# Stick-breaking attention of a hybrid decoder layer: weights as beta times a scanned product of (1 - beta), in place of sums of logarithms on TensorE

## The chip, the cores and the metric

One core of one Trainium2 chip runs the whole layer. The metric is the device time of one execution in microseconds (us). PE is TensorE, DVE is VectorE, ACT is ScalarE, POOL is GpSimd, SP is SyncE, which issues most loads.

## The reference, cut to what matters

The layer has three token mixers in parallel (sliding-window attention with 8 heads, stick-breaking attention with 8 heads, attention to a memory of 256 tokens), each with a sigmoid gate and a projection, then an output projection and a SwiGLU feed-forward. There are 512 tokens, width 1024, heads of 64. The change is in the second mixer (nb = 4 blocks of 128 queries):

```python
def stick_breaking_attention(q, k, v):
    """A[t,s] = beta_ts * prod_{s<j<t}(1-beta_tj), s<t."""
    ...
        z = jnp.einsum('bqhd,bkhd->bhqk', q[:, i * BLOCK:L], k[:, :L]).astype(jnp.float32) * (d ** -0.5)
        t = i * BLOCK + jnp.arange(BLOCK)[:, None]
        causal = jnp.arange(L)[None, :] < t
        log_1m = jnp.where(causal, jax.nn.log_sigmoid(-z), 0.0)
        between = lax.cumsum(log_1m, axis=3, reverse=True) - log_1m
        a = jnp.where(causal, jnp.exp(jax.nn.log_sigmoid(z) + between), 0.0)
        outs.append(jnp.einsum('bhqk,bkhd->bqhd', a.astype(v.dtype), v[:, :L]))
```

beta is the sigmoid of the score z. A query at t gives the key at s the weight beta(t,s) times the product of 1 - beta over all keys between s and t.

## The kernel before

Nearly all products are made in float32r, with each operand split into a high and a low part (`split`: ACT casts `raw` to `hi`, DVE subtracts to get `lo`); `mm3` issues hi x hi, hi x lo and lo x hi. `mm` issues a single product.

Two things are interleaved in the middle part of the program. One is the stream `dn`: a list of weight units (projections `ka`, `qa`, gates `g1`, queries `qm`, memory keys `pmk`, memory values `pmv`, branch projections `br`), each loaded 4 units ahead by SP, split 3 units ahead, and multiplied on PE by a generator that yields an estimated time after each `mm3`. The other is the attention heads, generators too, that yield how many us of the stream are to stand at this place: `for us in sb_head(h): dn.run(us)`. A scheduler then sets each engine's order; `tc.high_priority()` and `after` (an order between two instructions without a wait) steer it. `dn.until(flag)` runs the stream up to a mark. ACT's functions come in table sets; `table(name)` loads one, ordered behind all earlier `fn` calls, and later ones stand behind it.

A stick-breaking head before the change has keys on the partitions and queries along the free axis. There are 10 blocks of 128x128 under the causal mask, in three PSUM banks `z` (SEG and W give place and width). PE makes the scores and adds a mask of -1e30 (`negm`). ACT makes |z|, then exp, then ln(1 + ...), DVE adds max(z, 0): this is the softplus, the negative logarithm of 1 - beta. DVE splits it into `sh` and `sl`. After 7.0 us of stream, PE adds the sums over later keys into `z`: with a triangle of -1 (`ntri`) inside a block and with a square of -1 (`none`) for whole blocks. ACT takes exp, which gives the weights with the keys on partitions, as the product with the values needs them. After 3.0 us of stream, and for odd heads only, PE multiplies the weights of the head pair with the values into `ysb`, and `pair_out` splits the result.

All eight heads run with ACT's set of logarithm and exponential. Behind them the stream runs to the end of the branch's gates, `sigmoids(SB)` loads the sigmoid set, takes the sigmoid of the gates and the first set comes back for the sliding-window softmax.

Of the kernel before, what the change touches and what calls it, by code (L numbers as in the profile page):

```python
# [17 lines left out]
P = 128  # L18
# [85 lines left out]
def tile_kernel(ctx, tc, a):  # L104
# [62 lines left out]
    def mm3(out, l, r, start, stop, right_last=False):  # L167
        (lh, ll), (rh, rl) = l, r
        one = nc.tensor.matmul(out, lh, rh, start=start, stop=False, skip_group_check=True)  # L169
        two, three = ((ll, rh), (lh, rl)) if right_last else ((lh, rl), (ll, rh))  # L170
        nc.tensor.matmul(out, *two, start=False, stop=False, skip_group_check=True)  # L171
        return one, nc.tensor.matmul(out, *three, start=False, stop=stop, skip_group_check=True)  # L172
# [373 lines left out]
    def mem_keys(i):  # L546
        def gen(hi, lo):
            if i % 2 == 0:
                st[("mk", i // 2)] = ck(f"mk{i}")
            t = st[("mk", i // 2)][:, (i % 2) * M : (i % 2 + 1) * M]  # L550
            ps = dps(f"pmk{i}")
            for k in range(KC):
                mm3(ps[:, :M], cols((hi, lo), k * P, P), mu[k], k == 0, k == KC - 1)
                yield 0.325
            nc.vector.tensor_tensor(t, ps[:, :M], st["mrb"][:, :], op=ALU.mult)
            if i % 2 == 1:
                st[("mks", i // 2)] = parts(f"mks{i // 2}", st[("mk", i // 2)])

        return gen

    def mem_vals(q):
        def gen(hi, lo):
            if q == 0:
                st["mrs"] = per_token("m", st["mrb"], M, dps)
                st["pmv"] = [dps(f"pmv{t}") for t in range(2)]
            for i in range(2):
                k = 2 * q + i
                for t in range(2):
                    x = (mu[k][0][:, t * P : (t + 1) * P], mu[k][1][:, t * P : (t + 1) * P])
                    mm3(st["pmv"][t][:, :], x, cols((hi, lo), i * 512, 512), k == 0, k == KC - 1)  # L570
                    yield 0.65
                    if k == KC - 1:
                        vt = ck(f"mv{t}")
                        nc.vector.tensor_scalar(
                            vt[:, :], st["pmv"][t][:, :], st["mrs"][:, t : t + 1], None, op0=ALU.mult
                        )
                        st[("mvs", t)] = parts(f"mvs{t}", vt)

        return gen
# [153 lines left out]
    ntri = const("ntri", [P, P])  # L733
# [7 lines left out]
    ntri_r = cst.tile([P, P], F32R, name="ntri_r")  # L741
    nc.gpsimd.tensor_copy(ntri_r[:, :], ntri[:, :])
    none = cst.tile([P, P], F32, name="none")
    nc.gpsimd.memset(none[:, :], -1.0)
    none_r = cst.tile([P, P], F32R, name="none_r")
    nc.gpsimd.tensor_copy(none_r[:, :], none[:, :])
# [19 lines left out]
    def band_bias():  # L766
# [10 lines left out]
        )  # L777
        ps = aps("pbias")
# [15 lines left out]
        return out  # L794


    SEG = [(0, 0, 512), (1, 0, 384), (2, 0, 256), (2, 256, 128)]
    W = [512, 384, 384]
# [5 lines left out]
    def sb_head(h):  # L804
        c = h // 2
        ks, qs, ql = (st[(x, c, h % 2)] for x in ("kbs", "qbs", "qbl"))
        z = [aps(f"z{h}{i}") for i in range(3)]

        def seg(ts, j):
            i, o, n = SEG[j]  # L810
            return ts[i][:, o : o + n]

        for j in range(4):
            i, o, n = SEG[j]
            kj = slice(j * P, (j + 1) * P)
            if j < 3:
                out, qh, qlo = z[i][:, o : o + n], qs[:, j * P :], ql[:, j * P :]
            else:

                out = z[i][:, o : o + 2 * n]  # L820
                qh = qs[:, j * P :].unsqueeze(1).to_broadcast([P, 2, P])
                qlo = ql[:, j * P :].unsqueeze(1).to_broadcast([P, 2, P])
            mm(out, ks[:, kj], qh, j < 3, False)
            mm(out, ks[:, kj], qlo, False, False)
        for i, o, n in SEG:
            mm(z[i][:, o : o + P], identb[:, :], negm[:, :], False, False)
        e = [ck(f"e{h}{i}") for i in range(3)]
        sh = [ck(f"sh{h}{i}", F32R) for i in range(3)]
        sl = [ck(f"sl{h}{i}", F32R) for i in range(3)]
        for i in range(3):  # L830
            x, n = e[i][:, : W[i]], W[i]
            nc.scalar.activation(x, z[i][:, :n], AF.Abs)
# [3 lines left out]
            if i == 2:  # L836

                nc.vector.tensor_tensor(e[i][:, 384:], e[i][:, 128:256], e[i][:, 256:384], op=ALU.add)
                x, n = e[i][:, :], 512
            nc.vector.tensor_copy(sh[i][:, :n], x)  # L840
            nc.vector.tensor_tensor(sl[i][:, :n], x, sh[i][:, :n].bitcast(F32), op=ALU.subtract)
        yield 7.0

        def both(t):

            return t[2][:, :].rearrange("p (b n) -> p b n", b=4)[:, 0:4:3, :]
# [12 lines left out]
        for i in range(3):  # L859
            last = fn(e[i][:, : W[i]], z[i][:, : W[i]], AF.Exp)  # L860
        yield 3.0
        if h % 2 == 0:
            st["even"] = e
            return

        ys = aps(f"ysb{c}")
        for j in range(4):
            for i, x in enumerate((st["even"], e)):
                ins = mm(ys[64 * i : 64 * i + 64, j * P :], vcols(j, 128 + (2 * c + i) * 64), seg(x, j), j == 0, j == 3)
                after(ins, last)  # L870
                last = ins
        pair_out(SB, c, ys)

# [4 lines left out]
    def swa_pair(c, bias):  # L878
        hs = (c, c + 4)
        s, w, pt, pts = {}, {}, {}, {}  # L880
        for i, h in enumerate(hs):
            qs, ks, kl = st[("qas", c, i)], st[("kas", 0, i)], st[("kal", 0, i)]
            s[h] = [aps(f"s{h}{i}") for i in range(2)]
            for n in (1, 0, 2, 3):
                q = slice(n * P, (n + 1) * P)
                if n == 0:
                    kh = ks[:, :P].unsqueeze(1).to_broadcast([P, 2, P])
                    klo = kl[:, :P].unsqueeze(1).to_broadcast([P, 2, P])
                else:
                    keys = slice((n - 1) * P, (n + 1) * P)  # L890
                    kh, klo = ks[:, keys], kl[:, keys]
                mm(blocks(s[h], n), qs[:, q], kh, n in (1, 2), False)
                mm(blocks(s[h], n), qs[:, q], klo, False, True)
        for h in hs:
            b = bias[h // 2][:, (h % 2) * 256 : (h % 2) * 256 + 256]
            w[h] = [ck(f"w{h}{i}") for i in range(2)]
            nc.gpsimd.memset(w[h][0][:, :P], NEG)
            nc.vector.tensor_tensor(w[h][0][:, P:256], s[h][0][:, P:256], b[:, P:256], op=ALU.add)
            nc.vector.tensor_tensor(w[h][0][:, 256:], s[h][0][:, 256:], b, op=ALU.add)
            nc.vector.tensor_tensor(  # L900
                w[h][1][:, :].rearrange("p (n k) -> p n k", n=2),
                s[h][1][:, :].rearrange("p (n k) -> p n k", n=2),
# [19 lines left out]
        for h in hs:  # L922

            pt[h] = [aps(f"pt{h}{i}") for i in range(2)]
            for n in range(NT):
                for e in range(2):
                    j = n - 1 + e
                    if j < 0:
                        continue
# [3 lines left out]
            nc.scalar.copy(pts[h][0][:, :], pt[h][0][:, :])  # L933
            nc.vector.tensor_copy(pts[h][1][:, :384], pt[h][1][:, :384])
        yield 2.0
        ys = aps(f"ysw{c}")
        for j in range(NT):
            n = 256 if j < 3 else P
            for i, h in enumerate(hs):
                mm(ys[64 * i : 64 * i + 64, j * P : j * P + n], vcols(j, i * 64), blocks(pts[h], j)[:, :n], j == 0, j == 3)  # L940
# [50 lines left out]
    table("sigmoid_and_others")  # L991
    sigmoids(SB)
# [534 lines left out]
def _constants():  # L1527
# [16 lines left out]
def _layout(i):  # L1544
# [5 lines left out]
    x, mem = i["x"][0], i["mem"][0]  # L1550
# [57 lines left out]
```

## Time and profile before

| what | value |
|---|---|
| median of 3 runs | 806.78 us (806.52 to 806.88) |
| the profiled execution | 806.6 us |
| its span on the core | 804.8 us |
| granted TensorE clock | 0.998 |
| PE, DVE, ACT, POOL busy | 99%, 77%, 59%, 10% of the span |
| eight stick-breaking heads with the stream between | from about 79 to 208 us |

The profile page gives busy times, the chain of work that ended last and the costliest groups; answers of the trace give single instructions in order of time (start, duration), waits, and busy times by stretch. PE's instructions overlap: the time that one costs is read from its start to the start of the next.

### The profile page before, as it was taken

What the parts mean: (1) busy time and instruction counts of PE and PEld (TensorE: products, weight loads), DVE (VectorE), ACT (ScalarE), POOL (GpSimd) and SP (SyncE); (2) the same over time, 40 slices, a digit from 0 to 9 for tenths busy, and PEclk for the clock granted to TensorE, in tenths of its full rate; (3) what the DMA queues carried; (4) which work ended last, traced back from release to release, by engine and by line L of the source; (5) the groups of instructions that cost most, each with busy time, mean ns of one, the idle gap of its engine ahead of it and who ended that gap; (6) DMA issues with size and microseconds to landing.
All of it is one profiled execution on the core that took longest, in us unless ns stands there. A gap on an engine that the chain in (4) does not pass through costs nothing.

```text
span 804.8 us, 12915 instructions
## 1 busy us (share of the span) xinstructions
PE 795.6 (99%) x4939; PEld 708.2 (88%) x4939; DVE 616.2 (77%) x983; ACT 477.0 (59%) x861; POOL 78.9 (10%) x101
## 2 busy tenths in 40 slices
PE   9999999999999999999999999999999999999996
PEld 6899788878788889889988899999999999988885
DVE  6898678646377888796694779967676767898787
ACT  7466677666756555754662566554444444666673
POOL 1002210000000000100004200100000000205200
PEclk9999999999999999999999999999999999999999
DMA  9343355211241404704669927987777662859802
GB/s 320 118 148 105 125 176 149 87 53 53 80 105 53 106 26 133 182 27 132 187 234 305 224 45 172 257 222 205 190 176 191 174 167 69 190 129 225 204 2 104
DMA packets 41726, 117.68 MB, mean 146 GB/s; under 512 B 4768, under 2 KB 6320, under 8 KB 41664
## 3 DMA queue, kind: packets, MB, share of 16 engines
q1 hardware_dynamic: 31584, 87.77, 33.9%
q0 software_dynamic: 9648, 28.82, 19.2%
q8 instruction: 38, 0.62, 0.3%
q10 hardware_dynamic: 432, 0.27, 0.1%
q14 instruction: 24, 0.20, 0.1%
HBM read 113.18 MB, written 3.67 MB: 145 GB/s over the span
## 4 chain that ended last, share of the span: by engine, by line
PE 95%; DVE 2%; ACT 1%; issue 1%; DMA 1%; DVEq 0%; ACTq 0%
PE gx L172 5%; PE gx L169 5%; PE gx L171 5%; PE z L175 4%; PE g L169 3%; PE br L169 3%; PE br L171 3%; PE g L171 3%; PE g L172 3%; PE br L172 3%; PE x L172 2%; PE x L171 2%; PE x L169 2%; PE gy L171 2%; PE gy L169 2%; PE gy L172 2%
## 5 line engine op out<-in xcount | busy, mean ns | idle before, releaser
L135 ACT CAST hi<-gw 128x1024 fp32r<-128x1024 f32 x77 | 79.9, 1048 | 81.4 <-DVE gw L1193 39.8
L136 DVE TENSOR_TENSOR lo<-gw,hi 128x1024 fp32r<-128x1024 f32 x77 | 93.5, 1223 | 34.1 <-ACT hi L135 34.0
L135 ACT CAST hi<-raw 128x1024 fp32r<-128x1024 f32 (+2 forms) x52 | 53.0, 1031 | 50.8 <-PE qb L171 11.3
L136 DVE TENSOR_TENSOR lo<-raw,hi 128x1024 fp32r<-128x1024 f32 (+2 forms) x52 | 63.0, 1217 | 20.1 <-ACT hi L135 19.9
L1175 POOL DMA_DIRECT2D gw<-in_w_gu x27 | 23.3, 895 | 190.4 <-DMA gw<-in_w_gu 81.4
L135 ACT CAST hi<-r 128x1024 fp32r<-128x1024 f32 (+1 forms) x24 | 23.5, 981 | 19.9 <-PE y L172 5.3
L171 PE MATMUL x<-lo,lh 128*128 128x512 f32 x88 | 34.3, 389 | 0.0
L169 PE MATMUL x<-hi,lh 128*128 128x512 f32 x88 | 34.2, 389 | 0.0
L172 PE MATMUL x<-hi,ll 128*128 128x512 f32 x88 | 34.1, 389 | 0.0
L136 DVE TENSOR_TENSOR lo<-r,hi 128x1024 fp32r<-128x1024 f32 (+1 forms) x24 | 27.1, 1130 | 4.0 <-ACT hi L135 3.9
L135 ACT CAST hi<-qw 128x1024 fp32r<-128x1024 f32 x18 | 18.9, 1051 | 16.0 <-PE g L171 3.9
L136 DVE TENSOR_TENSOR lo<-qw,hi 128x1024 fp32r<-128x1024 f32 x18 | 21.9, 1219 | 8.4 <-ACT hi L135 8.4
L835 DVE SCALAR_TENSOR_TENSOR e<-z,e 128x384 f32<-128x384 f32 (+1 forms) x24 | 14.3, 598 | 17.7 <-ACT e L188 17.7
L188 ACT ACTIVATE e<-e 128x384 f32<-128x384 f32 (+1 forms) x48 | 26.9, 561 | 1.6
L135 ACT CAST hi<-bp 128x512 fp32r<-128x512 f32 x33 | 19.3, 620 | 13.6 <-PE y L172 4.8
L136 DVE TENSOR_TENSOR lo<-bp,hi 128x512 fp32r<-128x512 f32 x33 | 22.1, 702 | 5.7 <-ACT hi L135 5.6
L172 PE MATMUL gx<-N2h,lo 128*128 128x256 f32 x88 | 25.0, 284 | 0.3 <-DVE lo L136 0.3
L169 PE MATMUL gx<-B11h,hi 128*128 128x256 f32 x88 | 25.1, 285 | 0.2 <-ACT B11h L1104 0.2
L169 PE MATMUL mx<-woh,mgh 128*128 128x512 f32 x64 | 25.0, 391 | 0.0
L172 PE MATMUL gw<-B21h,lo 128*128 128x256 f32 x88 | 25.0, 284 | 0.0
L171 PE MATMUL gx<-B11l,hi 128*128 128x256 f32 x88 | 25.0, 284 | 0.0
L172 PE MATMUL mx<-woh,mgl 128*128 128x512 f32 x64 | 24.9, 390 | 0.0
(920 smaller groups left out, 2967.5 us busy)
## 6 DMA issues: line engine op xcount, KB each, us to landing
gw<-in_w_gu SPq DMA_DIRECT2D x57, 512.0 KB, 5.1
gw<-in_w_gu POOLq DMA_DIRECT2D x27, 512.0 KB, 7.4
raw<-in_w_p SPq DMA_DIRECT2D x26, 512.0 KB, 4.3
qw<-in_w_p SPq DMA_DIRECT2D x15, 512.0 KB, 4.1
raw<-in_w_br SPq DMA_DIRECT2D x12, 512.0 KB, 3.8
bp<-in_w_dn SPq DMA_DIRECT2D x22, 256.0 KB, 8.7
r<-in_w_dn POOLq DMA_DIRECT2D x10, 512.0 KB, 8.1
raw<-in_w_out SPq DMA_DIRECT2D x8, 512.0 KB, 4.4
```

The lines of the kernel that those rows point to most:

```text
L135: ins = nc.scalar.copy(hi, raw)
L136: lows = nc.vector.tensor_tensor(lo, raw, hi.bitcast(F32), op=ALU.subtract)
L169: one = nc.tensor.matmul(out, lh, rh, start=start, stop=False, skip_group_check=True)
L171: nc.tensor.matmul(out, *two, start=False, stop=False, skip_group_check=True)
L172: return one, nc.tensor.matmul(out, *three, start=False, stop=stop, skip_group_check=True)
L175: return nc.tensor.matmul(out, l, r, start=start, stop=stop, skip_group_check=True)
L188: ins = nc.scalar.activation(*args, **kw)
L835: nc.vector.scalar_tensor_tensor(x, z[i][:, :n], 0.0, x, op0=ALU.max, op1=ALU.add)
L1175: nc.gpsimd.dma_start(gw[(n, key)][:, :], g_src(n, i, j), accum_op=ALU.add)
```

## The change

Queries go on the partitions and keys along the free axis, and all tokens are stored last first (the input's rows are reversed on the host and the output's back). The keys before a query then stand to its right, nearest first, and the product over the keys between is a running product along the free axis.

- Scores: the same products with the sides swapped. The narrowest block, once made 256 wide by repeating its 128 columns, is now 128 wide. The mask stays.
- ACT makes r = sigmoid(-z) and b = sigmoid(z), straight from PSUM. DVE scans r into a running product `p` (`tensor_tensor_scan`: state times r, then the maximum with `anew`, which is 0 but for a 1 where the second block of a bank begins anew), and multiplies b by the product one column before.
- The weights now have queries on the partitions. PE transposes the ten blocks (`at`), ordered behind the last `mm3` of the stream piece ahead of them, and ACT and DVE copy them to SBUF with priority. The product with the values follows as before, last key block first.
- The triangle and the minus ones, `sh` and `sl`, and their products go.
- The sigmoid set is loaded ahead of head 0, once the stream has made the memory norm, whose logarithm and exponential need the other set. The gates of this branch are then evacuated from PSUM through the sigmoid at once.
- The relative bias of the sliding window is loaded at head 0 and spread out at head 2 instead of all at head 1; the window blocks are mirrored. Memory keys and values are evacuated with priority, and the stream's price for a product of the keys is 0.37 instead of 0.325.

```diff
-    SEG = [(0, 0, 512), (1, 0, 384), (2, 0, 256), (2, 256, 128)]
-    W = [512, 384, 384]
+    SEG = [(0, 0, 512), (1, 0, 384), (2, 0, 256), (1, 384, 128)]
+    W = [512, 512, 256]
+    KEYS = [(1, 384, 128), (2, 0, 256), (1, 0, 384), (0, 0, 512)]
...
-            mm(out, ks[:, kj], qh, j < 3, False)
-            mm(out, ks[:, kj], qlo, False, False)
...
-        for i in range(3):
-            x, n = e[i][:, : W[i]], W[i]
-            nc.scalar.activation(x, z[i][:, :n], AF.Abs)
-            fn(x, x, AF.Exp, scale=-1.0)
-            st["chain"] = fn(x, x, AF.Ln, bias=1.0)
-            nc.vector.scalar_tensor_tensor(x, z[i][:, :n], 0.0, x, op0=ALU.max, op1=ALU.add)
...
-            nc.vector.tensor_copy(sh[i][:, :n], x)
-            nc.vector.tensor_tensor(sl[i][:, :n], x, sh[i][:, :n].bitcast(F32), op=ALU.subtract)
+        for n in range(NT):
+            i, o, w = SEG[n]
+            for x, first in ((qs, n < 3), (ql, False)):
+                mm(z[i][:, o : o + w], x[:, n * P : (n + 1) * P], ks[:, n * P :], first, False)
+        for n in (0, 1, 3, 2):
+            i, o, w = SEG[n]
+            mm(z[i][:, o : o + P], identb[:, :], negm[:, :], False, n > 1 or n == 0)
+        for i, w in enumerate(W):
+            fn(r[i][:, :w], z[i][:, :w], AF.Sigmoid, scale=-1.0)
+        for i, w in enumerate(W):
+            st["chain"] = fn(b[i][:, :w], z[i][:, :w], AF.Sigmoid)
+        for i, w in enumerate(W):
+            o = P if i == 1 else 0
+            p = ck(f"p{h}{i}")
+            nc.vector.tensor_tensor_scan(p[:, :w], r[i][:, :w], anew[:, o : o + w], 1.0, op0=ALU.mult, op1=ALU.max)
+            nc.vector.tensor_tensor(b[i][:, 1:w], b[i][:, 1:w], p[:, : w - 1], op=ALU.mult)
         yield 7.0
...
-        for j in range(2):
-            for t in (sh, sl):
-                mm(seg(z, j), ntri_r[:, :], seg(t, j), False, False)
-        for t in (sh, sl):
-            mm(z[2][:, :384], ntri_r[:, :], t[2][:, :384], False, t is sl)
-        for t in (sh, sl):
-            mm(z[0][:, 128:], none_r[:, :], seg(t, 1), False, False)
-        for t in (sh, sl):
-            mm(z[0][:, 256:], none_r[:, :], both(t), False, t is sl)
-            mm(z[1][:, 128:384], none_r[:, :], both(t), False, t is sl)
-        mm(z[2][:, 128:256], none[:, :], seg(e, 3), False, True)
-        for i in range(3):
-            last = fn(e[i][:, : W[i]], z[i][:, : W[i]], AF.Exp)
+        for n in (0, 1, 3, 2):
+            i, o, _ = SEG[n]
+            for j in range(n, NT):
+                t, c, _ = KEYS[j]
+                last = nc.tensor.transpose(
+                    pt[t][:, c + n * P : c + (n + 1) * P], b[i][:, o + (j - n) * P : o + (j - n + 1) * P], ident[:, :]
+                )
+                after(last, st["product"])
+        with tc.high_priority():
+            nc.scalar.copy(at[0][:, :], pt[0][:, :])
+            nc.vector.tensor_copy(at[1][:, :], pt[1][:, :])
+            nc.scalar.copy(at[2][:, :256], pt[2][:, :256])
         yield 3.0
...
+    while "mrb" not in st:
+        dn.piece()
+    table("sigmoid_and_others")
+    sigmoids(SB)
     for h in range(8):
-        if h == 1:
-            bias = band_bias()
+        if h == 0:
+            biases = band_bias()
+        if h in (0, 2):
+            bias = next(biases)
         for us in sb_head(h):
             dn.run(us)
     st.pop("chain")
     dn.until(f"gates{SB}")
-    table("sigmoid_and_others")
-    sigmoids(SB)
     table("natural_log_exp_and_others")
```

The order on three engines shows it. First PE in the second half of head 3, after the 7.0 us of stream. Before (`z_1427` to `z_1429` are the three score banks; moving operand first, then the stationary one):

```order
L175 MATMUL z_1427<-sh_1445,ntri_r 128x512
L175 MATMUL z_1427<-sl_1448,ntri_r 128x512
L175 MATMUL z_1428<-sh_1446,ntri_r 128x384
L175 MATMUL z_1428<-sl_1449,ntri_r 128x384
L175 MATMUL z_1429<-sh_1447,ntri_r 128x384
L175 MATMUL z_1429<-sl_1450,ntri_r 128x384
L175 MATMUL z_1427<-sh_1446,none_r 128x384
L175 MATMUL z_1427<-sl_1449,none_r 128x384
L175 MATMUL z_1427<-sh_1447,none_r 128x256
L175 MATMUL z_1428<-sh_1447,none_r 128x256
...
L175 MATMUL z_1429<-e_1444,none 128x128
L169 MATMUL qa_1527<-n0h,hi_1414 128x512
```

With the change (`at` are the turned weights in PSUM, `b` the weights):

```order
L172 MATMUL qa_1504<-n2h,lo_1399 128x512
L835 MATMUL at_1515<-c_ident,b_1429 128x128
L835 MATMUL at_1516<-c_ident,b_1429 128x128
L835 MATMUL at_1515<-c_ident,b_1429 128x128
L835 MATMUL at_1514<-c_ident,b_1429 128x128
L835 MATMUL at_1516<-c_ident,b_1430 128x128
L835 MATMUL at_1515<-c_ident,b_1430 128x128
L835 MATMUL at_1514<-c_ident,b_1430 128x128 x2
L835 MATMUL at_1515<-c_ident,b_1431 128x128
L835 MATMUL at_1514<-c_ident,b_1431 128x128
L169 MATMUL qa_1504<-n3h,hi_1398 128x512
```

Ten transposes stand where thirteen products stood (two of these, with `sl`, are left out above). Those that read the third weight tile come last.

Second, DVE in head 1. Before (`lo` is a weight's low part; `e` the softplus):

```order
L835 SCALAR_TENSOR_TENSOR e_1086<-z_1071,e_1086 128x512
L840 CAST sh_1089<-e_1086 128x512
L841 TENSOR_TENSOR sl_1092<-e_1086,sh_1089 128x512
L835 SCALAR_TENSOR_TENSOR e_1087<-z_1072,e_1087 128x384
L840 CAST sh_1090<-e_1087 128x384
L841 TENSOR_TENSOR sl_1093<-e_1087,sh_1090 128x384
L835 SCALAR_TENSOR_TENSOR e_1088<-z_1073,e_1088 128x384
L838 TENSOR_TENSOR e_1088<-e_1088 128x128
L840 CAST sh_1091<-e_1088 128x512
L136 TENSOR_TENSOR lo_1125<-raw_1002,hi_1124 128x1024
L841 TENSOR_TENSOR sl_1094<-e_1088,sh_1091 128x512
```

With the change (the scans are the rows that write `p`; `mk` are the memory keys):

```order
L826 SCALAR_TENSOR_TENSOR p_1103<-r_1094,anew 128x512
L826 SCALAR_TENSOR_TENSOR p_1106<-r_1095,anew 128x512
L827 TENSOR_TENSOR b_1091<-b_1091,p_1103 128x511
L827 TENSOR_TENSOR b_1092<-b_1092,p_1106 128x511
L826 SCALAR_TENSOR_TENSOR p_1109<-r_1096,anew 128x256
L136 TENSOR_TENSOR lo_1135<-raw_1057,hi_1134 128x1024
L557 TENSOR_TENSOR mk_1138<-pmk_1139,rb_m 128x256
L827 TENSOR_TENSOR b_1093<-b_1093,p_1109 128x255
```

Three scans and three products take the place of ten passes; a weight's low part and the memory keys stand ahead of the third product.

Third, ACT ahead of head 0. Before (`v_all` are the values, `t_m` and `rb_m` the memory norm):

```order
L508 COPY v_all<-pv_727 128x320
L832 ACTIVATE e_917<-z_902 128x512
L188 ACTIVATE e_917<-e_917 128x512 x2
L832 ACTIVATE e_918<-z_903 128x384
L188 ACTIVATE e_918<-e_918 128x384 x2
L832 ACTIVATE e_919<-z_904 128x384
L188 ACTIVATE e_919<-e_919 128x384 x2
L135 CAST hi_947<-raw_837 128x1024
L135 CAST hi_1004<-raw_945 128x1024
L188 ACTIVATE t_m<-ss_m,eps_t 128x256
L188 ACTIVATE rb_m<-t_m 128x256
```

With the change:

```order
L509 COPY v_all<-pv_722 128x320
L135 CAST hi_899<-raw_832 128x1024
L189 ACTIVATE t_m<-ss_m,eps_t 128x256
L189 ACTIVATE rb_m<-t_m 128x256
L197 ACT_TABLE_LOAD
L189 ACTIVATE r_955<-z_937 128x512
L189 ACTIVATE r_956<-z_938 128x512
L189 ACTIVATE r_957<-z_939 128x256
L189 ACTIVATE b_952<-z_937 128x512
L189 ACTIVATE b_953<-z_938 128x512
L189 ACTIVATE b_954<-z_939 128x256
```

The memory norm and a table load moved ahead of head 0's functions.

More of the change, by code (lines that the diff above doesn't have):

```diff
@@ L171, in mm3 @@
         nc.tensor.matmul(out, *two, start=False, stop=False, skip_group_check=True)
-        return one, nc.tensor.matmul(out, *three, start=False, stop=stop, skip_group_check=True)
+        st["product"] = nc.tensor.matmul(out, *three, start=False, stop=stop, skip_group_check=True)
+        return one, st["product"]
     def mm(out, l, r, start, stop):
@@ L740, in tile_kernel @@
     nc.gpsimd.tensor_copy(negm[:, :], nmf[:, :])
[L741 to L746, printed above, removed]
+    anew = cst.tile([P, 640], F32, name="anew")
+    nc.gpsimd.memset(anew[:, :], 0.0)
+    nc.gpsimd.memset(anew[:, 512:513], 1.0)
     def normed(k):
@@ L793, in band_bias @@
             out.append(b)
[L794 to L798 removed]
+        yield out
+    SEG = [(0, 0, 512), (1, 0, 384), (2, 0, 256), (1, 384, 128)]
+    W = [512, 512, 256]
+    KEYS = [(1, 384, 128), (2, 0, 256), (1, 0, 384), (0, 0, 512)]
     def pair_out(b, c, ps):
@@ L804, in sb_head @@
     def sb_head(h):
-        c = h // 2
-        ks, qs, ql = (st[(x, c, h % 2)] for x in ("kbs", "qbs", "qbl"))
+        c0 = h // 2
+        ks, qs, ql = (st[(x, c0, h % 2)] for x in ("kbs", "qbs", "qbl"))
         z = [aps(f"z{h}{i}") for i in range(3)]
[L809 to L822, printed above, removed]
-            mm(out, ks[:, kj], qh, j < 3, False)
-            mm(out, ks[:, kj], qlo, False, False)
@@ new lines, in sb_head @@
+        b = [ck(f"b{h}{i}") for i in range(3)]
+        r = [ck(f"r{h}{i}") for i in range(3)]
+        for i, w in enumerate(W):
[7 more added lines that the diff above has]
+            nc.vector.tensor_tensor(b[i][:, 1:w], b[i][:, 1:w], p[:, : w - 1], op=ALU.mult)
@@ new lines, in sb_head @@
+        yield 7.0
+        pt = [aps(f"at{h}{i}") for i in range(3)]
+        at = [ck(f"a{h}{i}") for i in range(3)]
+        for n in (0, 1, 3, 2):
[4 more added lines that the diff above has]
+                    pt[t][:, c + n * P : c + (n + 1) * P], b[i][:, o + (j - n) * P : o + (j - n + 1) * P], ident[:, :]
+                )
+                after(last, st["product"])
+        with tc.high_priority():
+            nc.scalar.copy(at[0][:, :], pt[0][:, :])
+            nc.vector.tensor_copy(at[1][:, :], pt[1][:, :])
+            nc.scalar.copy(at[2][:, :256], pt[2][:, :256])
@@ L861, in sb_head @@
         yield 3.0
         if h % 2 == 0:
-            st["even"] = e
+            st["even"] = at
             return
[L866 to L869, printed above, removed]
+        ys = aps(f"ysb{c0}")
+        for j in range(NT - 1, -1, -1):
+            t, c, n = KEYS[j]
+            for i, x in enumerate((st["even"], at)):
+                ins = mm(
+                    ys[64 * i : 64 * i + 64, :n], vcols(j, 128 + (2 * c0 + i) * 64), x[t][:, c : c + n], j == 3, j == 0
+                )
@@ L883, in swa_pair @@
             s[h] = [aps(f"s{h}{i}") for i in range(2)]
-            for n in (1, 0, 2, 3):
+            for n in range(NT):
                 q = slice(n * P, (n + 1) * P)
-                if n == 0:
-                    kh = ks[:, :P].unsqueeze(1).to_broadcast([P, 2, P])
-                    klo = kl[:, :P].unsqueeze(1).to_broadcast([P, 2, P])
+                if n == 3:
+                    kh = ks[:, q].unsqueeze(1).to_broadcast([P, 2, P])
+                    klo = kl[:, q].unsqueeze(1).to_broadcast([P, 2, P])
                 else:
-                    keys = slice((n - 1) * P, (n + 1) * P)
+                    keys = slice(n * P, (n + 2) * P)
                     kh, klo = ks[:, keys], kl[:, keys]
-                mm(blocks(s[h], n), qs[:, q], kh, n in (1, 2), False)
+                mm(blocks(s[h], n), qs[:, q], kh, n in (0, 2), False)
                 mm(blocks(s[h], n), qs[:, q], klo, False, True)
@@ L932, in swa_pair @@
             pts[h] = [ck(f"pts{h}{i}") for i in range(2)]
-            nc.scalar.copy(pts[h][0][:, :], pt[h][0][:, :])
-            nc.vector.tensor_copy(pts[h][1][:, :384], pt[h][1][:, :384])
+            nc.vector.tensor_copy(pts[h][0][:, P:], pt[h][0][:, P:])
+            nc.scalar.copy(pts[h][1][:, :], pt[h][1][:, :])
         yield 2.0
@@ L937, in swa_pair @@
         for j in range(NT):
-            n = 256 if j < 3 else P
+            o = 0 if j else P
             for i, h in enumerate(hs):
-                mm(ys[64 * i : 64 * i + 64, j * P : j * P + n], vcols(j, i * 64), blocks(pts[h], j)[:, :n], j == 0, j == 3)
+                mm(
+                    ys[64 * i : 64 * i + 64, (j - 1) * P + o : (j + 1) * P],
+                    vcols(j, i * 64), blocks(pts[h], j)[:, o:], j == 0, j == 3
+                )
         pair_out(SWA, c, ys)
@@ L1606 @@
     r = run_bass_kernel_spmd(nc, [ins], core_ids=[0])
-    return r.results[0]["out_0"].reshape(1, S, D)
+    return np.ascontiguousarray(r.results[0]["out_0"][::-1]).reshape(1, S, D)
```

45 lines of the change are left out of this document (17 added, 28 removed).

## The prediction

> **What bounds the kernel now.** I read the page first: busy time of the engines, then the chain of work that ended last.
>
> ```profile
> span 804.8 us, 12915 instructions
> PE 795.6 (99%) x4939; PEld 708.2 (88%) x4939; DVE 616.2 (77%) x983; ACT 477.0 (59%) x861; POOL 78.9 (10%) x101
> ...
> PE 95%; DVE 2%; ACT 1%; issue 1%; DMA 1%; DVEq 0%; ACTq 0%
> ```
>
> PE is 99% busy and 95% of the chain. Busy time is not proof of a full PE, since ends are modelled, so the second view is who PE waits for (us in total, times, longest; these two rows are the only ones behind the warm-up but for two of 0.2 elsewhere), the third the stage that the change touches, the eight stick-breaking heads, in stretches of a head or so each (the first, the last, and the sum of eight):
>
> ```profile
> PE gx L172 <- DVE lo L136: 0.3, 1, 0.3
> ...
> PE z L175 <- DVE sl L841: 0.2, 1, 0.2
> ```
>
> ```profile
> 79.20:95.50 16.30, 16.11 (x81) 13.20 (x79) 13.64 (x23) 11.71 (x22) 4.47 (x8) 1.00 0.37 113
> ...
> 192.40:208.50 16.10, 16.10 (x86) 12.48 (x85) 7.34 (x12) 12.00 (x21) 0.41 (x2) 1.00 0.23 66
> sum 128.50, PE 128.29 PEld 105.91 DVE 83.16 ACT 88.92 POOL 8.68; mean PE 16.04 PEld 13.24 DVE 10.39 ACT 11.12 POOL 1.09
> ```
>
> In 128.5 us of heads PE is idle 0.2 us, DVE is busy 83 and ACT 89, at the full granted clock (1.00). So a microsecond of PE work taken out here is a microsecond of the kernel, as long as no new wait comes; a microsecond taken from ACT or DVE is worth nothing by itself. I cost PE from one start to the next, since the durations overlap.
>
> **Removed from PE.** Per head, the products with the triangle and with the minus ones (12 in two-part precision, one in plain f32 that shows as two records), and the 256-wide form of the narrow score block. Head 0, then head 3, in order of time (start, duration):
>
> ```profile
> 80.30 0.28 PE L175 MATMUL z<-qbs,kbs 128*128 128x256 f32 x1
> 80.42 0.29 PE L175 MATMUL z<-qbl,kbs 128*128 128x256 f32 x1
> 80.54 0.40 PE L175 MATMUL z<-negmb,identb 128*128 128x128 bf16 x4
> 80.75 0.48 PE L169 MATMUL ka<-n0h,hi 128*128 128x512 f32 x1
> 81.07 0.39 PE L171 MATMUL ka<-n0l,hi 128*128 128x512 f32 x1
> 81.30 0.40 PE L172 MATMUL ka<-n0h,lo 128*128 128x512 f32 x1
> ...
> 87.22 0.39 PE L175 MATMUL z<-sh,ntri_r 128*128 128x512 f32 x1
> ...
> 89.67 0.40 PE L169 MATMUL qa<-n0h,hi 128*128 128x512 f32 x1
> ...
> 91.74 0.38 PE L175 MATMUL z<-e,none 128*128 128x128 f32 x2
> 91.87 0.48 PE L169 MATMUL qa<-n3h,hi 128*128 128x512 f32 x1
> 92.19 0.39 PE L171 MATMUL qa<-n3l,hi 128*128 128x512 f32 x1
> ...
> 137.00 0.39 PE L175 MATMUL z<-sh,ntri_r 128*128 128x512 f32 x1
> ...
> 139.13 0.48 PE L169 MATMUL qa<-n0h,hi 128*128 128x512 f32 x1
> 139.45 0.39 PE L171 MATMUL qa<-n0l,hi 128*128 128x512 f32 x1
> ```
>
> An undisturbed 512-wide product takes 0.23 (81.07 to 81.30). The first one behind the f32 product takes 0.32 (91.87 to 92.19), so 0.09 of the f32 product shows up in its successor. Head 3's set: 137.00 to 139.13 is 2.13, plus 0.09: 2.22. Head 0's: 87.22 to 89.67 is 2.45 (a wait in it), plus 0.13 and 0.09: 2.67. The chain of waits shows the set of heads 3 and 6, in one piece each, the third row being a set of transposes in the sliding-window part:
>
> ```profile
> 137.16 2.21 PE z L175 x14
> ...
> 186.48 2.52 PE z L175 x14
> ...
> 229.74 1.53 PE pt L931 x14
> ```
>
> So 2.2 where nothing disturbs and up to 2.7 where the parts come late. The mean of 2.67, 2.22 and 2.52 would be 2.47; since disturbed heads weigh too much in these three, I take 2.35, midway between it and the undisturbed 2.22. The narrow block's pair costs 0.24 (80.30 to 80.54). Removed: 2.59 a head.
>
> **Added to PE.** Ten f32 transposes of 128x128 a head: 1.53/14 = 0.109 each by the row above, 1.09. The narrow block as two 128-wide products, a form that no row has. Below, the 128-wide bf16 mask: 80.54 to 80.75 for four, 0.05 each. Above, the plain f32 product of that shape: 0.13 + 0.09 = 0.22. A narrow two-part product can't be dearer than full f32. Its nearest row by operands is the 256-wide pair, 0.12 each, which by columns would give 0.06; by shape and element size it is the f32 product. I take 0.22, the value against the change, so 0.44; 0.05 to 0.22 stays in the range. The other score products only swap the sides of the operands, with the same widths; the masks, and the products with the values (taken in the reverse order of key blocks), keep number and widths.
>
> Net: 2.59 - 1.09 - 0.44 = 1.06 us a head, **8.5 us for eight heads**. With 0.05 instead of 0.22 it is 11.2; with 2.22 instead of 2.35, 7.4.
>
> **ACT.** Twelve passes a head become six sigmoids and two copies. It waits for nothing on the path that I can shorten, so this earns nothing; what counts is when its results arrive (below). The eight gates of this branch are now evacuated through the sigmoid, which takes out eight copies, 592 ns in the row below (min, median, max): nothing on PE, since it waits for none of them. Table loads keep their number; one moves ahead of head 0. The gate copies, POOL's sums for the memory norm, then PE, ACT, and the table loads as a group (busy, mean ns):
>
> ```profile
> L304 ACT ACTIVATE g<-g x8: 588/592/593, 169.9 to 217.7; 128x512 f32<-128x512 f32 x8
> ```
>
> ```profile
> 77.98 2.67 POOL L539 TENSOR_TENSOR mT<-mT,mT 128x512 f32<-128x512 f32 x2 [1.09 <-ACT mT L535]
> ```
>
> ```profile
> 79.19 0.39 PE L175 MATMUL z<-qbs,kbs 128*128 128x512 f32 x1
> ...
> 82.91 1.02 PE L175 MATMUL ss_m<-mT,ones 128*128 128x256 f32 x4
> 83.58 0.58 PE L169 MATMUL ka<-n3h,hi 128*128 128x512 f32 x1
> ```
>
> ```profile
> 88.15 0.47 ACT L188 ACTIVATE t_m<-ss_m,eps_t 128x256 f32<-128x256 f32 x1
> 88.65 0.42 ACT L188 ACTIVATE rb_m<-t_m 128x256 f32<-128x256 f32 x1
> ```
>
> ```profile
> L196 ACT ACT_TABLE_LOAD x8 | 10.3, 1283 | 0.1
> ```
>
> The memory norm's sum (ss_m) now stands before head 0's scores, nine products after the last value product, which ends where head 0's scores begin in this row, so at 79.19 + 9 x 0.23 = 81.3. Its input leaves POOL at 80.65, so PE has 0.6 us to spare. Then 0.67 for ss_m, 0.2 on the way, 0.47 + 0.42 for logarithm and exponential, 1.28 for the table: ACT is ready for sigmoids at 84.4. Head 0's scores start three products later, at 82.7, and their masks end at 84.4. The table load just fits; if it slips, head 0's chain slips with it, for which it has 1 us of room (next part).
>
> **The chain inside a head.** This is where PE could wait: scores, sigmoids, scan, product, transposes. Rows that price it (head 2):
>
> ```profile
> 115.17 0.60 ACT L832 ACTIVATE e<-z 128x512 f32<-128x512 f32 x1 [0.97 <-PE z L175]
> ...
> 120.00 2.94 ACT L135 CAST hi<-raw 128x1024 fp32r<-128x1024 f32 x3
> ```
>
> ```profile
> 116.10 0.42 DVE L555 TENSOR_TENSOR mk<-pmk,rb_m 128x256 f32<-128x256 f32 x1 [1.18 <-PE pmk L172]
> ...
> 118.32 0.69 DVE L841 TENSOR_TENSOR sl<-e,sh 128x512 fp32r<-128x512 f32 x1
> ...
> 121.64 1.22 DVE L136 TENSOR_TENSOR lo<-raw,hi 128x1024 fp32r<-128x1024 f32 x1
> ```
>
> Filler on PE between masks and first transpose, by the built order: 33 products of 512 in head 0 (7.5 us), 12 of 512 and 33 of 256 in head 1 (2.7 + 4.0 = 6.7 us), 6.8 to 8.1 us in the others. Take head 1, the tightest, with 0 at the end of its masks. ACT: three r at 0.63, 0.63, 0.45 until 1.8, three b until 3.5, then the cast that DVE waits for, until 4.5. DVE's queue reads scan, scan, product, product, scan, the weight's low part, the memory keys' product, and last the third product.
>
> The scan has no row. Below, a two-input pass over 512: 0.69. Above, the same over 1024 columns, as if each column took two steps: 1.22 (dearer yet is a rival). A recurrence has to have one column's result before the next, so I take the upper one. With 1.22: scans until 3.2, two products (0.69) until 4.6, third scan (0.69) until 5.3, low part (1.22) until 6.5, memory keys (0.42) until 6.9, third product (0.42) until 7.3. PE reaches the transposes at 6.7 and those of the third tile, the last two of ten, at 6.7 + 8 x 0.109 = 7.6. Room: 0.3 us in head 1, about 1.1 in most others, which lack the memory keys' product and have 7.5 us of filler. With 0.69 it ends at 6.5: room 1.1. So by either end I cost the chain at nothing, hidden by the projections' products; head 1 may pay some tenths.
>
> [...]
>
> DVE per head: before 0.69 + 2 x 0.55, casts and subtractions, about 5.2; after, scans 3.1, products 1.8, one copy 0.6: 5.5. Of 16 us a head DVE was busy 10.4, so it stays far from full. The copies of the turned weights are wanted only 2.7 us or more of filler later, and only in odd heads.
>
> **The rest, with one answer.** The bias rows are read back a head later; before, POOL issued them at 104, and the first scores that want them ran at 217:
>
> ```profile
> 104.12 2.90 POOL L792 DMA_DIRECT2D bias<-bscr  x4 [5.94 <-PE qa L172]
> ```
>
> ```profile
> 216.91 1.91 PE s L175 x16
> ```
>
> A head is 16 us, so some 95 us of room stay. The mirrored window blocks keep counts and widths. The earlier evacuation of the memory keys and values shortens nothing that PE waits for. The load of the triangle and the casts at the start go; PE read those only in the heads. Reversing the tokens is done outside the device.
>
> **Sum.** The profiled execution took 806.6 (804.8 span), the runs shown have a median of 806.78, 0.2 above. 806.8 - 8.5 = 798.3; with 0.3 for small new waits in heads 0 and 1, **798.6**.
>
> **Rivals.**
> - *The narrow products run at their columns' pace* (0.05 to 0.12): 795.6 to 796.7. For it: the 256-wide row scales so. Against: nothing narrower of this kind is in the trace.
> - *The scan is so slow that every head waits* (the other side). In the heads without the memory keys' product, with scan time S for 512, the third product ends at 3.84 + 2.57 S, and PE is there at 8.4: waiting starts at S = 1.8, eats the whole gain of 1.06 a head at S = 2.2, and at S = 2.5 costs 1.9 a head: 8 x 1.9 - 8.5 = 6.5 slower, 813. For it: no row of a scan. Against: that is 3.6 times the 512-wide pass.
> - *Part of it*: S near 2.0, or ACT's evacuations getting in front of the sigmoids: 0.4 to 0.7 a head, 801 to 804, still faster or even.
> - *The transposes cost what f32 products cost* (0.22): ten are 2.2, the net falls to nothing: 806.5. Against: the fourteen in 1.53 us.
>
> **How the numbers follow.** The forecast has 0.68, the fast narrow products 0.14, the partial wait 0.09, the dear transposes 0.03, the slow scan 0.06. A change under 0.2% (1.6 us) can hardly be told from none here. Faster: 0.68 + 0.14 + 0.05 of the partial wait = 0.87; same 0.03 of the partial wait + 0.03 of the dear transposes = 0.06; slower 0.06 + the last 0.01 of the partial wait = 0.07. The range reaches from the fast narrow products, 795.6, to the start of the partial wait, 802.0.
>
> **What would show it.** Right: about 80 transposes starting 0.11 apart in the heads, no products with the triangle, PE without a wait in that stage, a stage about 8.5 us shorter and everything behind it shifted by that much. The 128-wide score products: 0.22 apart, or less. The scan: 1.2 us. Wrong: PE's transposes (at) waiting for DVE's third product in most heads, or ss_m waiting for POOL.

## The result, and the profile after

The changed kernel takes 799.03 us (median of four runs, 798.86 to 800.47) against 806.77 (806.52 to 806.88): a ratio of 0.9908 (0.9891 to 0.9926), 7.7 us faster. The forecast was 798.6 with a range of 795.6 to 802.0. The profiled execution took 799.01. Two executions of one kernel below, the one without the priority, took 1111 and 2761 us, far longer than its other eight, and are left out of its numbers. Its page, busy times first and then the shares of the chain of work that ended last:

```profile
PE 786.1 (99%) x4907; PEld 699.0 (88%) x4907; DVE 618.4 (78%) x959; ACT 452.0 (57%) x821; POOL 79.9 (10%) x100
...
PE 94%; DVE 3%; issue 1%; ACT 1%; DMA 1%; DVEq 0%; ACTq 0%
```

PE still bounds the kernel, but DVE's share of the chain went from 2% to 3%. Why, the view of PE's waits shows (us in total, times, longest):

```profile
PE pmv L169 <- DVE rs_m L241: 1.2, 1, 1.2
PE qa L169 <- DVE mv L577: 1.0, 1, 1.0
PE st_m L239 <- DVE mk L557: 0.3, 1, 0.3
```

None of them is the stick-breaking heads' own. All three are in the stream between heads, where the memory keys (`mk`), the norm column (`rs_m`) and the memory values (`mv`) are evacuated from PSUM. In stretches, with the columns as in the prediction, the loss shows up behind the first head only:

```profile
79.20:95.50 16.30, 16.30 (x84) 13.81 (x83) 13.89 (x20) 11.78 (x21) 4.88 (x8) 1.00 0.38 113
95.50:200.80 105.30, 102.77 (x582) 83.67 (x582) 69.77 (x90) 54.89 (x98) 4.22 (x7) 1.00 0.37 115
```

PE idles 2.5 us in the second stretch (105.30 less 102.77); before it was 0.2 in all eight heads. The clock stays at 1.00.

The place of the longest wait, first PE, then DVE, in order of time:

```profile
118.63 0.44 PE L239 MATMUL st_m<-c_ident,rb_m 128*128 128x128 f32 x2 [0.34 <-DVE mk L557]
...
122.23 0.50 PE L169 MATMUL pmv<-hi,mh 128*128 128x512 f32 x1 [1.16 <-DVE rs_m L241]
```

```profile
118.17 0.73 DVE L557 TENSOR_TENSOR mk<-pmk,rb_m 128x256 f32<-128x256 f32 x2
118.82 0.41 DVE L827 TENSOR_TENSOR b<-b,p 128x255 f32<-128x255 f32 x1
119.15 1.22 DVE L136 TENSOR_TENSOR lo<-raw,hi 128x1024 fp32r<-128x1024 f32 x1
120.28 0.69 DVE L136 TENSOR_TENSOR mks1l<-mk,mks1h 128x512 fp32r<-128x512 f32 x1
120.89 1.22 DVE L136 TENSOR_TENSOR lo<-raw,hi 128x1024 fp32r<-128x1024 f32 x1
122.02 0.15 DVE L241 COPY rs_m<-st_m 128x2 f32<-128x2 f32 x1
```

`st_m` (the memory norm, turned so that it can be copied out as the column `rs_m`) is in PSUM by 119.1. Its copy takes 0.15 us but stands behind a product and three subtractions, until 122.02. The stream's products use a pool of two banks (`psd`), so the second `pmv` tile can't start before `st_m`'s bank is free.

The heads themselves are as forecast. The transposes and scans (min, median, max in ns), then head 0's scores on PE and its first functions on ACT:

```profile
L835 PE MATMUL at<-c_ident,b x80: 270/273/273, 91.9 to 196.3; 128*128 128x128 f32 x80
```

```profile
L826 DVE TENSOR_TENSOR_SCAN p<-r,anew x24: 681/1199/1227, 85.3 to 191.9; 128x512 f32<-128x512 f32 x16, 128x256 f32<-128x256 f32 x8
```

```profile
83.82 0.28 PE L176 MATMUL z<-kbs,qbl 128*128 128x256 f32 x1
83.94 0.22 PE L176 MATMUL z<-kbs,qbs 128*128 128x128 f32 x1
84.00 0.27 PE L176 MATMUL z<-kbs,qbl 128*128 128x128 f32 x1
84.11 0.40 PE L176 MATMUL z<-negmb,identb 128*128 128x128 bf16 x4
...
91.90 1.25 PE L835 MATMUL at<-c_ident,b 128*128 128x128 f32 x10
92.91 0.48 PE L169 MATMUL qa<-n7h,hi 128*128 128x512 f32 x1
```

```profile
83.34 1.28 ACT L197 ACT_TABLE_LOAD   x1
84.63 1.36 ACT L189 ACTIVATE r<-z 128x512 f32<-128x512 f32 x3
```

The two narrow products take 0.17 us from start to the mask behind them (83.94 to 84.11), where the prediction put 0.44. Ten transposes take 1.01 to the next start (91.90 to 92.91), plus 0.09 in the successor.

### The profile page after: what moved, and what is told of

Its sections match the earlier page's. It is cut to its first block, busy times and chain, and to the rows that moved or that the text cites. A ratio compares the mean times of both kernels' runs of the same rounds, so it can differ in the third digit from the quotient of the medians.

```text
span 797.2 us, 12790 instructions
## 1 busy us (share of the span) xinstructions
PE 786.1 (99%) x4907; PEld 699.0 (88%) x4907; DVE 618.4 (78%) x959; ACT 452.0 (57%) x821; POOL 79.9 (10%) x100
## 4 chain that ended last, share of the span: by engine, by line
PE 94%; DVE 3%; issue 1%; ACT 1%; DMA 1%; DVEq 0%; ACTq 0%
PE gx L172 5%; PE gx L169 5%; PE gx L171 5%; PE g L169 3%; PE g L172 3%; PE br L169 3%; PE br L171 3%; PE g L171 3%; PE br L172 3%; PE x L169 3%; PE x L172 3%; PE x L171 3%; PE gy L171 2%; PE gy L169 2%; PE gy L172 2%; PE mx L172 2%
## 5 line engine op out<-in xcount | busy, mean ns | idle before, releaser
L826 DVE TENSOR_TENSOR_SCAN p<-r,anew 128x512 f32<-128x512 f32 (+1 forms) x24 | 24.2, 1036 | 12.4 <-ACT r L189 12.4
L172 PE MATMUL gy<-T1h,lo 128*128 128x256 f32 x88 | 24.9, 283 | 0.0
```

Source lines behind the costliest of these rows:

```text
L172: st["product"] = nc.tensor.matmul(out, *three, start=False, stop=stop, skip_group_check=True)
L826: nc.vector.tensor_tensor_scan(p[:, :w], r[i][:, :w], anew[:, o : o + w], 1.0, op0=ALU.mult, op1=ALU.max)
```

## The experiments

The theory at this point: PE is full, so PE work taken out counts in full, and what is missing from the forecast's better end is lost in waits for PSUM banks whose evacuations stand late on DVE. Rivals: the scan or the transposes hold the heads up, or the narrow products cost what f32 products do.

### The transposes, twice

```diff
-                last = nc.tensor.transpose(pt[t][...], b[i][...], ident[:, :])
+                for _twice in range(2):
+                    last = nc.tensor.transpose(pt[t][...], b[i][...], ident[:, :])
```

> The changed kernel with each of the 80 transposes issued twice. Theory (PE bound, 0.109 each): 8.7 us more, 807.7, and the second set starts 0.109 apart. Rival (PE stands in wait for DVE at these places, so that some of the added work is covered): the waits of PE for DVE in heads 2 and 3, about 2.5 us, shrink and the time rises by 6 us or less, to 805.

Measured: 807.36 us, 8.3 more than the changed kernel, 0.104 for each of the 80 added ones, near the first expectation. PE's waits are the same. The term of 1.09 a head stands, and PE work in this stage is paid in full.

### The scans, twice

```diff
             nc.vector.tensor_tensor_scan(p[:, :w], r[i][:, :w], anew[:, o : o + w], 1.0, ...)
+            nc.vector.tensor_tensor_scan(p[:, :w], r[i][:, :w], anew[:, o : o + w], 1.0, ...)
```

> The changed kernel with each scan done twice, so 3.1 us more on DVE in every head. Theory (the chain inside a head has about 1 us of room): the third product ends 3.1 later, PE waits for it about 1.7 to 2 us in each head, 8 heads give 13 to 16 us, so 812 to 815, with PE waiting in the transposes for DVE b. Rival (the filler covers the chain whatever the scan costs): under 802.

Measured: 812.27 us, 13.2 more, inside what was expected. PE's longest waits, in the profiled execution (810.86):

```profile
PE at L836 <- DVE b L828: 3.6, 4, 1.1
PE st_m L239 <- DVE mk L557: 2.6, 1, 2.6
PE qa L169 <- DVE mv L577: 2.1, 1, 2.1
```

So the heads do wait once the scan work doubles, but only 3.6 us of it is at the transposes, where 13 to 16 were expected: the time was met, its place was not. More is lost at the stream's own banks: these two waits and three smaller ones make 8.9 us. A scan that takes once its time holds up no transpose.

### The memory norm's column and the values evacuated by ACT

```diff
-        nc.vector.tensor_copy(rs[:, :], pt[...])
+        with tc.high_priority():
+            nc.scalar.copy(rs[:, :], pt[...])
...
-                            nc.vector.tensor_scalar(vt[:, :], st["pmv"][t][:, :], st["mrs"][...], None, op0=ALU.mult)
+                            nc.scalar.activation(vt[:, :], st["pmv"][t][:, :], AF.Identity, scale=st["mrs"][...])
```

> The changed kernel with two evacuations moved from DVE to ACT: the column of the memory norm (rs_m) and the memory values (mv). Theory (what the gain lacks is PE waiting in heads 2 and 3 for these evacuations, queued on DVE behind the scans, since the next product needs their PSUM bank): the waits of 1.2 and 1.0 us go, 796.5 to 797.0. Rival (the waits only move to the next thing that DVE or ACT is late with): 798.5 to 799.5, with other waits of the same sum in these heads.

Measured: 796.78 us, 2.25 less than the changed kernel and within the first expectation; against the kernel before a ratio of 0.9877 (0.9862 to 0.9891). Of the three waits there are left:

```profile
PE st_m L239 <- DVE mk L558: 0.3, 1, 0.3
PE qa L169 <- ACT mv L578: 0.2, 1, 0.2
```

The waits of 1.2 and 1.0 are gone, and their sum less the 0.2 that is left is 2.0 of the 2.25 us. The theory of late evacuations holds.

### Without the priority of these evacuations

```diff
-                yield 0.37
-            with tc.high_priority():
+                yield 0.325
+            if True:
...
-                        with tc.high_priority():
+                        if True:
```

> The changed kernel without the priority of the memory keys' and values' evacuation and with the old price of 0.325 in the stream (that part of the change undone). Theory (PE waits where such an evacuation is late on DVE behind the scans): without priority it is later, PE waits 1 to 4 us more in heads 1 to 3, 800 to 803. Rival, as the prediction had it (priority shortens nothing that PE waits for): 799.0 within 0.3.

Measured: eight executions from 802.61 to 806.40 us, with a median of 805.5, and a ratio of 0.9974 (0.9962 to 0.9986). That is 6.4 us more than the changed kernel; only the quickest of the eight lies within the first expectation, and none within the rival's. The profiled one took 806.26. Waits, then PE behind the first two and behind the last of them, then the granted clock (the column behind POOL's busy time):

```profile
PE qa L169 <- DVE mv L577: 3.4, 1, 3.4
PE pmv L169 <- DVE mk L557: 1.4, 1, 1.4
PE st_m L239 <- DVE mk L557: 1.4, 1, 1.4
```

```profile
121.35 0.80 PE L169 MATMUL pmv<-hi,mh 128*128 128x512 f32 x1 [1.36 <-DVE mk L557]
121.95 0.63 PE L171 MATMUL pmv<-lo,mh 128*128 128x512 f32 x1
122.37 0.63 PE L172 MATMUL pmv<-hi,ml 128*128 128x512 f32 x1
...
127.07 0.52 PE L171 MATMUL pmv<-lo,mh 128*128 128x512 f32 x1
...
141.35 0.76 PE L169 MATMUL qa<-n0h,hi 128*128 128x512 f32 x1 [3.40 <-DVE mv L577]
...
144.05 0.55 PE L169 MATMUL qa<-n2h,hi 128*128 128x512 f32 x1
```

```profile
122.00:124.00 2.00, 2.00 (x6) 1.60 (x5) 1.10 (x3) 0.00 (x0) 1.95 (x3) 0.50 0.93 254
```

This is a second price of a wait. Behind two waits of 1.36 that only two transposes part, and again behind one of 3.4, the granted clock is 0.50, and 512-wide products start 0.43 apart (12 of them from 121.95 to 127.07) in place of 0.23. That costs 5.72 less 13 x 0.23, 2.7 us, up to 127.07, and 2.70 less 6 x 0.23, 1.3, up to 144.05. The three waits above are 6.2 us long, against 2.5 of the changed kernel's three: 3.7 more. Together this makes 7.7; the profiled executions differ by 7.25. The mean clock was 0.999 in the quickest execution (802.61) and 0.991 to 0.994 in the six slowest (804.90 to 806.40), so the price in clock is not the same each time.

Without the priority of these evacuations, and with the stream price of 0.37 undone alongside, most of the gain is gone: 6.4 of 7.7 us. This run does not separate the two, and the price also shifts some of the stream's products on PE.

How long one wait is does not alone decide this. Each of the two waits of 1.36 is shorter than the one of 2.6 us with the doubled scans, and behind that one the clock did not fall in the profiled execution: the stretch with that wait (122 to 124 us) and all those around it have 1.00. The last section sets rows of both kinds side by side.

### The old sums, left out and doubled

Two kernels on the program before. The first leaves the thirteen products out, the second issues each twice (one line of the products is shown for each):

```diff
-            mm(z[0][:, 256:], none_r[:, :], both(t), False, t is sl)
...
-            last = fn(e[i][:, : W[i]], z[i][:, : W[i]], AF.Exp)
+            last = fn(e[i][:, : W[i]], z[i][:, : W[i]], AF.Exp, scale=0.01)
```

> The kernel before, without the thirteen products a head with the triangle and the minus ones (it leaves out the sums over later keys, so its weights are not the stick-breaking ones; the exponential takes 0.01 z to stay finite). Theory (PE is the bound, a microsecond of PE is a microsecond of time): the removed term alone, 2.35 a head by the prediction, is 18.8 us, so 788.0; 2.22 a head would give 789.0. Rival (the PE time taken out comes back as waits for DVE or ACT, whose work is unchanged): 792 or more, with PE waits of several us in the heads.

```diff
+            mm(z[0][:, 256:], none_r[:, :], both(t), False, False)
             mm(z[0][:, 256:], none_r[:, :], both(t), False, t is sl)
```

> The kernel before with each of the thirteen products a head with the triangle and the minus ones issued twice (the sums over later keys count double). Theory (PE bound, the set costs 2.35 a head as the prediction took it, 2.22 undisturbed): 17.8 to 18.8 us more, 824.6 to 825.6. Rival (the first experiment's slowdown means that these products partly fill time in which PE would wait anyway): 820 or less.

Doubled: 822.89 us, 16.0 more, 2.0 a head, with no new wait; this lies between the two expectations. Left out: 817.84, 11 us *slower* with 17.9 us of PE work gone (start to start, in the trace before), the opposite of what was expected. In the profiled execution (815.62) PE is busy for 786.6 us of a span of 813.8. The view of waits, and one instruction of ACT in head 0:

```profile
PE st_m L238 <- DVE mk L555: 4.5, 1, 4.5
PE qa L169 <- DVE v_m L216: 4.3, 1, 4.3
PE g L169 <- ACT g L304: 4.2, 3, 2.2
PE pmk L169 <- ACT qa L304: 4.2, 1, 4.2
```

```profile
84.55 0.60 ACT L188 ACTIVATE e<-z 128x512 f32<-128x512 f32 x1 [1.01 <-DVE sl L841]
```

With nothing on PE to wait for, the scheduler put each last exp of the head earlier in ACT's queue, where it waits for DVE, and the evacuations behind it come late. The waits of those four rows and one of 1.3 are 18.5 us: they eat the whole gain. Then the clock falls as well, here in one stretch of 20 us, to a mean of 0.83 with PE busy for 15.53:

```profile
120.00:140.00 20.00, 15.53 (x98) 13.60 (x95) 13.44 (x23) 12.73 (x23) 0.00 (x0) 0.83 0.31 96
```

As a test of what the products cost, this run failed, since it also moved ACT's order. It shows something else: in this program, where an evacuation stands in its queue can be worth as much as all the PE work that the change removes.

### Five narrow products instead of one

Each of the two 128-wide score products a head is issued five times:

```diff
-                mm(z[i][:, o : o + w], x[:, ...], ks[:, ...], first, False)
+                for _more in range(5 if n == 3 else 1):
+                    mm(z[i][:, o : o + w], x[:, ...], ks[:, ...], first, False)
```

> The changed kernel with the pair of 128-wide score products issued five times instead of once in each head, 64 products more in all (the scores of that block come out five times too large). Theory after the first trace (these products run at their columns' pace, 0.06 each): 64 x 0.06 = 3.8 us, 802.9. Rival, the term as the prediction took it (0.22, as plain f32): 64 x 0.22 = 14.1, 813.1.

Measured: 805.89 us, 6.9 more for 64 added products: 0.107 each, between the two theories. Head 0 (ten in the two groups, then the mask):

```profile
83.77 0.67 PE L176 MATMUL z<-kbs,qbs 128*128 128x128 f32 x5
84.27 0.72 PE L176 MATMUL z<-kbs,qbl 128*128 128x128 f32 x5
84.84 0.40 PE L176 MATMUL z<-negmb,identb 128*128 128x128 bf16 x4
```

Ten in 1.07 us. The first of a row takes 0.06 (behind a 256-wide one, in the rows of the result, half of that one's 0.12), each further one about 0.11, hardly less than a 256-wide product's 0.12 (83.82 to 83.94 there). Neither theory had that.

### The weights turned in float32r

On the version with ACT's evacuations, the transposes read the weights as float32r. In the first kernel the product goes to new tiles `br`, and POOL copies column 0:

```diff
-            nc.vector.tensor_tensor(b[i][:, 1:w], b[i][:, 1:w], p[:, : w - 1], op=ALU.mult)
+            nc.vector.tensor_tensor(br[i][:, 1:w], b[i][:, 1:w], p[:, : w - 1], op=ALU.mult)
+            nc.gpsimd.tensor_copy(br[i][:, 0:1], b[i][:, 0:1])
```

> The kernel of the fourth experiment (memory evacuations on ACT) with the weights written as float32r and turned in that type (they are rounded to it). Theory (a 128-wide float32r product starts 0.06 after the one before it, and a turn of that type too): 80 x (0.109 - 0.06) = 3.9 us less than 796.8, so 792.9. Rival (a turn goes by element size or by its weight load, 0.109 whatever the type): 796.8, the transposes still 0.109 apart.

Measured: 807.23 us, 10.4 more than the version that it is built on, and above both expectations. The transposes are indeed shorter (247 ns), but look at the waits and what follows the longest:

```profile
L840 PE MATMUL at<-ident_r,br x80: 222/247/252, 91.9 to 204.6; 128*128 128x128 f32 x80
```

```profile
PE st_m L239 <- DVE mk L558: 3.2, 1, 3.2
PE g L169 <- ACT g L189: 2.8, 2, 1.4
PE qa L169 <- ACT mv L578: 1.7, 1, 1.7
```

```profile
123.65 0.63 PE L171 MATMUL pmv<-lo,mh 128*128 128x512 f32 x1
124.08 0.63 PE L172 MATMUL pmv<-hi,ml 128*128 128x512 f32 x1
```

PE's order is that of the version it is built on. ACT's and DVE's orders differ in many places: casts of weights moved ahead of products and gate evacuations. Behind the wait of 3.2, PE's products again start 0.43 apart (123.65 to 124.08), at a granted clock of 0.51 from 124 to 126 us. Whether the float32r form itself cost anything was open, so the second kernel keeps the weights in place; ACT's and DVE's orders differ from those of the version with ACT's evacuations in three places only:

```diff
-        b = [ck(f"b{h}{i}") for i in range(3)]
+        b = [ck(f"b{h}{i}", F32R) for i in range(3)]
...
-            nc.vector.tensor_tensor(b[i][:, 1:w], b[i][:, 1:w], p[:, : w - 1], op=ALU.mult)
+            nc.vector.tensor_tensor(b[i][:, 1:w], b[i][:, 1:w].bitcast(F32), p[:, : w - 1], op=ALU.mult)
```

> The kernel e4_mem_act with the weights kept as float32r in the place where they already lie: the second sigmoid writes b as float32r, the product by the scan overwrites it, and the transposes read it with a float32r identity. No instruction is added on any queue but one copy of the identity on POOL at the start; TensorE's order is that of e4 and e8, and ACT's and DVE's orders differ from e4's by three casts in all, where e8's differ in many places. If TensorE sets the time and e8 lost its gain only to the order on ACT and DVE: 796.8 - 80 x (0.109 - 0.084) = 794.8 us (794.3 to 795.4), with transposes 0.084 apart and the waits of e4. If the float32r form itself costs something around the transposes (a wait of the first one, a slower evacuation of the turned weights): 796.5 or more, with PE waiting at those lines.

Measured: 794.94 us (794.82 to 795.10), ratio 0.9851 (0.9834 to 0.9869), the best of all versions, 4.1 us below the changed kernel and within the first expectation.

```profile
91.98 0.96 PE L838 MATMUL at<-ident_r,b 128*128 128x128 f32 x10
92.78 0.46 PE L169 MATMUL qa<-n7h,hi 128*128 128x512 f32 x1
```

Ten transposes take 0.80 to the next start, against 1.01: 1.7 us in eight heads, of 1.84 measured. So no cost of the float32r form shows. The other kernel's 10 us are in its waits, 9.9 us more than in the version that it is built on and none of them at the transposes. That the changed order of two queues made them, and not POOL's copies, is likely but not shown by a run of its own.

## Why the prediction was right, point by point

The main mechanism was right: PE bounds the stage, and the time fell by about the net PE work. That the forecast came within 0.5 us of the result is in part luck: one term was too dear by 2.2 us, and the new waits were 2.2 us longer than forecast, and these two offset each other.

- **Removed sums, 2.35 a head.** Right in the mean, and in part by luck. From start to start in the trace before, with what the f32 product adds to its successor, the set costs 2.67 in head 0, about 2.5 in heads 1 and 2 and 2.22 in heads 3 to 7: 2.34 on average. The row that the prediction took for head 6's set (186.48, 2.52) is something else: from 186.31 to 187.90 come nine of its products, then until 188.84 five score products of head 7. So the 2.47 was a mean over a misread row, and the midpoint happened to fall on the true mean. Doubling the products added 2.0 a head, less than the set costs; by an estimate from the rows of before, part of the gap is the 0.09 in the successor, paid only once there.
- **Transposes, 1.09 a head.** Right: 1.01 and 0.09, and 0.104 for each one added.
- **Narrow products, 0.44 a head.** Too dear: 0.17. The choice of 0.22 against 0.05 was the wrong nearest row for the first of a pair (0.06) and twice too dear for the second (0.11). Worth 8 x 0.27 = 2.2 us in favour. By this term alone, the rival of narrow products at their columns' pace (0.05 to 0.12) was right.
- **New waits, 0.3 in heads 0 and 1.** Wrong in place and size: 2.5 in the stretch behind head 0, at the memory norm's column, keys and values. The failed step is the sentence that the earlier evacuation of memory keys and values "shortens nothing that PE waits for". It looked at who waited before; with the new order on DVE they are what PE waits for first. Taking that evacuation's priority away, with the stream price, costs 6.4 us; giving the norm's column and the values to ACT earns 2.25. The sum had nothing for the priority, so it would have been the same without it, and 805.5 lies outside its range.
- **Sum.** 8.5 and 2.2, less 2.5, is 8.2; measured is 7.7. Most of the half microsecond left is in the memory values' 48 products (`pmv`): they take 11.7 us from start to start without the waits, against 11.0 before, for those next to a wait or a transpose start 0.3 to 0.4 apart.
- **The scan, 1.22.** Right: 1.20 at the median, 0.68 for 256 columns, and no transpose waits for it. 256 more columns cost the scan 0.52 (1.20 less 0.68), and a two-input pass 0.27 (0.69 less 0.42): each further column took the scan 1.9 times as long, near the upper end's two steps. The rivals of a slow scan and of a partial wait in the heads did not come.
- **Head 0.** The table load ended at 84.62 and the first sigmoid began at 84.63, with the masks issued from 84.11 on: as close as forecast (84.4), and without loss. The 0.2 that the prediction put between PE's part of the norm and ACT's logarithm, an estimate without a row, was 0.38 (82.01, where PE's next product starts, to 82.39).
- **Dear transposes** did not come.

## What to carry to other kernels

When PE is full, an edit's PE work can be summed from start to start (here 0.104 for each added transpose, against 0.109 by the rows), but ask also which evacuations share the queue that gets the new work: an engine that is 78% busy on average here still delayed a 0.15 us copy by 3 us, since four others stood ahead of it, and with a pool of two PSUM banks PE stood too. Before costing a priority at nothing, look at who would wait in the new order, not at who waits now. An experiment that takes work out is only read as that work's price once the orders on the other engines are seen to be the same.

## What the runs showed of the hardware that was not expected

A wait of PE can cost more than its length: behind the wait of 3.40 us in the kernel without the priority and that of 3.16 us in the first float32r kernel, 512-wide products started 0.43 apart instead of 0.23 for 2.1 us (141.91 to 144.05 and 123.65 to 125.78), at a granted clock of 0.50 and 0.51. The length of one wait alone does not decide it. In the kernel without the priority, two waits of 1.36 with two transposes between them were followed by a clock of 0.50 too; with the doubled scans, one of 2.6 was not. Here are stretches around that one, then around the wait of the first float32r kernel (PE's busy time comes first, the granted clock behind POOL's):

```profile
120.00:122.00 2.00, 1.74 (x15) 1.53 (x13) 2.00 (x2) 0.84 (x2) 0.00 (x0) 1.00 1.02 376
122.00:124.00 2.00, 0.00 (x0) 0.00 (x0) 2.00 (x5) 0.70 (x1) 0.49 (x1) 1.00 0.17 61
124.00:126.00 2.00, 1.69 (x8) 1.34 (x9) 2.00 (x4) 0.62 (x1) 2.00 (x4) 1.00 0.55 135
126.00:128.00 2.00, 1.21 (x6) 0.66 (x4) 2.00 (x4) 0.00 (x0) 0.41 (x1) 1.00 0.88 272
```

```profile
118.00:120.00 2.00, 1.57 (x14) 1.36 (x12) 2.00 (x3) 0.84 (x2) 0.00 (x0) 1.00 1.01 373
120.00:122.00 2.00, 0.00 (x0) 0.00 (x0) 2.00 (x4) 0.53 (x1) 0.59 (x1) 1.00 0.77 205
122.00:124.00 2.00, 1.27 (x4) 1.12 (x5) 1.26 (x5) 0.68 (x2) 2.00 (x4) 0.63 0.79 221
124.00:126.00 2.00, 2.00 (x6) 1.53 (x5) 0.43 (x1) 0.00 (x0) 0.72 (x4) 0.51 1.00 387
126.00:128.00 2.00, 2.00 (x16) 1.70 (x15) 0.00 (x0) 0.55 (x1) 0.00 (x0) 1.00 0.77 283
```

What else decides it, and why the mean clock differs between executions of the kernel without the priority (0.991 to 0.999), these runs do not show.

In the kernel with five narrow products, a further 128-wide float32r product in a row of its kind cost 0.107 us (6.9 us for 64), nearly what a 256-wide one did (0.12). Transposes of 128x128 in float32r cost 0.08 each (ten in 0.80 us) against 0.10 in f32 (ten in 1.01).
